# The FFN's first product: every second group of channel tiles by seven block products, activations stationary

## The chip, the cores and the metric

One core of a Trainium2 chip. Its engines run side by side: TensorE (PE in the profile: matmuls; PEld: their weight loads), VectorE (DVE), ScalarE (ACT), GpSimd (POOL) and SyncE (SP, which here only issues transfers from the chip's memory). Each engine executes its own queue of instructions in order; an instruction that needs another engine's result waits at the head of its queue. The metric is the device time of one execution in microseconds: before the change the median of three runs is 1574.26 us (1574.19 to 1574.32).

## The reference, cut to what matters

One layer over 256 tokens of width 2048, in float32. A mixer (recurrent branch, attention, pooling, gates) yields `merged`; then

```
x = x + merged @ w_out
h2 = rms_norm(x, g_ffn)                      # x / rms(x) * g_ffn, per token
gate, up = split(h2 @ w_ffn_in, 2)           # 2048 -> 2 x 5632 channels
x = x + (silu(gate) * up) @ w_ffn_out        # 5632 -> 2048
return rms_norm(x, g_final)
```

Only the part from `w_out` to the end is touched.

## The kernel before

All activations are kept transposed, [128 channels of a tile, 256 tokens]. Products must be near float32 accurate, so each operand is taken as two parts of about 12 bits, `hi` and `lo`, that PE multiplies at full rate, and three of the four partial products are summed: hi.hi, hi.lo, lo.hi.

A weight comes as a piece of 1 MB (`load`, into one of three buffers `raw`). `split` (L69, L70) makes the two parts of 1024 columns of it: ACT casts to `whi`, DVE subtracts to `wlo`; four such pairs of part buffers exist (`hl`), and splits are given priority over up to 200 earlier instructions (`AHEAD`), which fixes where they stand in the queues. In `mm_t` (L82, L83) the weight parts are stationary, 128 x 128 at a time, and the activations move: one matmul of 512 columns (hi and lo of 256 tokens side by side) and one of 256. `mm_n` (L91 to L93) writes the same sum as three matmuls of 256 columns into one half of a bank. `evac_t` adds the two halves of a `mm_t` result (ACT copy L100, DVE add L101).

The order of the stages: v and forget logits; queries, keys and attention; the other branches; gates and merge (`mT`, the merged activations in two parts); out projection (16 tiles, each followed by the residual add and by h2, L578, L579, without the norm's factor, which is applied later); the FFN's first product, 44 channel tiles, each a gate block and an up block of 16 x 128 x 128 (88 loads of `wffi`); the down projection, 16 tiles of 44 x 128 x 128; the last norm, and the store of the result. The norm's factor R2 comes from `rsqrt_mean` (a chain of small operations) and multiplies gate (DVE, L601) and up (POOL, L604); L605 to L607 form the product and its two parts, `act`, for all 44 tiles.

The v stage (L263 to L265) is the one place where activations are stationary and weights move, in blocks of 344 columns. In attention, four transpositions by the identity stand between other products (L338).

Of the kernel before, what the change touches and what calls it, by code (L numbers as in the profile page):

```python
# [7 lines left out]
F32 = mybir.dt.float32  # L8
# [20 lines left out]
GATES = (2, 2, 2, 4)  # merge gates taken between the groups of the two branches  # L29
WARM = 8  # products of constants that run while the first loads are under way  # L30
# [8 lines left out]
def block_kernel(ctx: ExitStack, tc: tile.TileContext, xT, vec,  # L39
# [5 lines left out]
    raw_p = ctx.enter_context(tc.tile_pool(name="raw", bufs=3))  # L45
    hl_p = ctx.enter_context(tc.tile_pool(name="hl", bufs=4))
    acc_p = ctx.enter_context(tc.tile_pool(name="acc", bufs=4, space=bass.MemoryType.PSUM))
    aux_p = ctx.enter_context(tc.tile_pool(name="aux", bufs=4, space=bass.MemoryType.PSUM))
    hT_p = ctx.enter_context(tc.tile_pool(name="hT", bufs=1))
    sm = ctx.enter_context(tc.tile_pool(name="sm", bufs=2))  # L50

# [34 lines left out]
    # the same in columns 0..255 alone: a longer product, a shorter way out  # L86
# [8 lines left out]
    def evac_t(ps, dst, scale=1.0):  # L95
        """Adds the two halves of a transposed product, times scale, into dst [128, 256]."""
# [25 lines left out]
    vhl = at_p.tile([P, 2, 2, DB], F32R, name="vhl", bufs=1)  # token tile, part, channel  # L122
# [5 lines left out]
    warm = aux()  # keeps the array clocked up until the first operands are there  # L128
# [3 lines left out]
    def prepare_x(k):  # L132
        """Contraction tile k of x * g_mix as two parts, and its share of the sum of squares."""
# [12 lines left out]
    def rsqrt_mean(dst, ss, n, pool, nm):  # L146
        """dst (or two factors of it) = (ss / D + eps) ** -0.5, with one Newton step behind the table's root."""
# [45 lines left out]
    for c in (0, 2):  # keep where query >= key  # L193
# [109 lines left out]
    def scores(h, q, k):  # L303
        """Softmax of head h's scores, transposed: [keys 0 | queries 0, 1], [keys 1 | queries 1]."""
# [10 lines left out]
        ns = at_p.tile([P, 3 * P], F32, name="ns")  # minus the scores  # L315
        st = at_p.tile([P, 8], F32, name="st")  # minus the maxima, sums, their reciprocals
# [77 lines left out]
    def lru_in(g):  # L394
# [22 lines left out]
        # gelu(y) = y (1 + tanh(c (y + 0.044715 y^3))) / 2  # L417
# [8 lines left out]
    def lru_out(g, u, uh, ul, ga):  # L426
# [14 lines left out]
        # th = tanh(-log(a) / 2): 1 - a = 2 th / (1 + th), 1 - a^2 = (1 - a)(1 + a).  # L441
# [7 lines left out]
        V.scalar_tensor_tensor(rg, rg, 2.0, rc, ALU.mult, ALU.mult)  # 1 - a  # L449
# [18 lines left out]
    def pool_in(g):  # L468
# [6 lines left out]
        # sums over 2, 4, 8, 16 tokens, each from the one before; column c holds token c - PADW  # L475
# [6 lines left out]
        # the mean, less the token itself: the first tokens count what there is  # L482
# [29 lines left out]
    def gate(n):  # L512
        """Sigmoid of gate block n = 3 m + branch."""
# [21 lines left out]
    mx_p.release()  # L535
    mT_p = tc.alloc_tile_pool(name="mT", bufs=1)
# [23 lines left out]
    h2 = hT_p.tile([P, KD, 2 * T], F32R, name="hT")  # [hi | lo] of x2 * g_ffn, transposed  # L560
# [22 lines left out]
    sg_p.release()
    yAC_p.release()
    yB_p.release()

# [1 line left out]
    ac_p = tc.alloc_tile_pool(name="act", bufs=1)  # L588
    act = ac_p.tile([P, NF, 2 * T], F32R, name="act")
    for f in range(NF):  # L590
        pg = proj_t(wffi[2 * f], lambda k: h2[:, k, :])
        pu = proj_t(wffi[2 * f + 1], lambda k: h2[:, k, :])
        if f == 0:
            ps = aux()
            PE.matmul(ps[:, :T], lhsT=ones, rhs=s2acc, start=True, stop=True)
            R2 = const.tile([P, T], F32, name="R2")
            rsqrt_mean(R2, [ps[:, :T]], T, sm, ("t0", "t1"))
        gt = sm.tile([P, T], F32, name="t0")
        up = sm.tile([P, T], F32, name="t1")
        evac_t(pg, gt)  # L600
        V.tensor_mul(gt, gt, R2)  # L601
        S.activation(gt, gt, AF.Silu)
        evac_t(pu, up)
        G.tensor_mul(up, up, R2)  # L604
        V.tensor_mul(gt, gt, up)  # L605
        S.copy(act[:, f, :T], gt)
        V.tensor_sub(act[:, f, T:], gt, act[:, f, :T].bitcast(F32))  # L607

# [4 lines left out]
    for m in range(KD):  # L613
        ps = acc()
        for a in range(0, NF, 16):
            n = min(16, NF - a)
            r = load(wffo[m, :, a * P:(a + n) * P], n * P)
            for c in range(0, n, 8):
                nk = min(8, n - c)
# [7 lines left out]
                (mm_n if m == last else mm_t)(ps, hi, lo, lambda k, k0=k0: act[:, k0 + k, :], nk,  # L627
                                              k0 == 0, k0 + nk == NF)
        g_ = vecs[:, GL + m:GL + m + 1]
        if m < last:  # L630
            o = sm.tile([P, T], F32, name="t0")
            evac_t(ps, o)
# [93 lines left out]
```

## Time and profile before

| | us |
|---|---|
| median of the runs | 1574.26 |
| span of the profiled execution | 1572.5 |
| first FFN product, 818.4 to 1312.2 | 493.8 |
| down projection, 1312.2 to 1559.4 | 247.2 |
| tail behind the last product, 1559.4 to 1572.5 | 13.1 |

The profile is one execution. Busy shares are of that span, and PE's counts the pipelined matmuls, whose ends are modelled. The profiled execution's own time is its span with 1.8 us around it, taking the runs' median for it. In the chain of what ended last, each step is followed back to what released it.

### The profile page before, as it was taken

To read this page: it belongs to the slowest core of one execution; us is meant where nothing else is said; L and a number is where in the kernel's file an instruction comes from. 1 tells how busy PE (TensorE), PEld (TensorE's weight loads), DVE (VectorE), ACT (ScalarE), POOL (GpSimd) and SP (SyncE) were. 2 spreads that over 40 slices of the span, in tenths; PEclk is the share of its full clock that TensorE was granted. 3 is DMA by queue.
4 is the path that set the end of the run, shared out by engine and by line. 5 is a ranking of instruction groups with operands and counts; after the bars stand their busy time and mean duration, and the time that the engine had idled before them with its cause. 6 is when DMAs were issued, how large, how long until landed. Compare 5 with 4: busy or idle time off the path is not lost.

```text
span 1572.5 us, 22842 instructions
## 1 busy us (share of the span) xinstructions
PE 1549.3 (99%) x8948; PEld 1362.1 (87%) x8948; DVE 994.3 (63%) x1356; ACT 821.3 (52%) x1264; POOL 154.8 (10%) x210
## 2 busy tenths in 40 slices
PE   8999999999999999999999999999999999999997
PEld 8888888888888888888888888888888888888886
DVE  9776677787565656667776555555555555445453
ACT  6565566666444444445555444444444444444442
POOL 7400011102000000000110000000000000010100
PEclk9999999999999999999999999999999999999998
DMA  7444455545555455555555555555555555555552
GB/s 245 170 155 159 140 184 185 212 164 200 185 190 197 167 202 184 201 174 201 188 188 183 189 189 189 188 188 188 188 188 187 188 188 178 188 196 178 192 187 88
DMA packets 46764, 288.92 MB, mean 184 GB/s; under 512 B 5184, under 2 KB 8000, under 8 KB 15936
## 3 DMA queue, kind: packets, MB, share of 16 engines
q1 hardware_dynamic: 46080, 286.54, 52.5%
q8 instruction: 70, 1.15, 0.3%
q10 hardware_dynamic: 576, 0.92, 0.2%
q14 instruction: 38, 0.31, 0.1%
HBM read 285.34 MB, written 2.10 MB: 183 GB/s over the span
## 4 chain that ended last, share of the span: by engine, by line
PE 93%; DVE 2%; POOL 2%; issue 2%; ACT 1%; DMA 0%; SPq 0%; DVEq 0%; POOLq 0%; ACTq 0%
PE acc L82 59%; PE acc L83 30%; POOL xn L232 1%; POOL part L144 1%; DVE wlo L70 1%; ACT whi L69 0%; POOL lev L479 0%; PE acc L91 0%; PE acc L93 0%; PE acc L92 0%; DVE xt L657 0%; PE aux L338 0%; DVE lma L179 0%; PE acc L264 0%; DMA raw<-in_wvf 0%
## 5 line engine op out<-in xcount | busy, mean ns | idle before, releaser
L82 PE MATMUL acc<-hT,whi 128*128 128x512 f32 x2800 | 983.6, 395 | 0.4 <-DVE hT L579 0.4
L70 DVE TENSOR_TENSOR wlo<-raw,whi 128x1024 fp32r<-128x1024 f32 (+2 forms) x554 | 671.3, 1213 | 476.5 <-ACT whi L69 475.5
L69 ACT CAST whi<-raw 128x1024 fp32r<-128x1024 f32 (+2 forms) x554 | 567.9, 1026 | 614.2 <-PE acc L82 425.1
L83 PE MATMUL acc<-hT,wlo 128*128 128x256 f32 x2800 | 785.6, 281 | 0.0
L82 PEld LDWEIGHTS acc<-hT,whi 128*128 128x128 f32 x2800 | 526.3, 188 | 122.2 <-DVE hT L579 0.7
L83 PEld LDWEIGHTS acc<-hT,wlo 128*128 128x128 f32 x2800 | 527.2, 188 | 0.2
L82 PE MATMUL acc<-act,whi 128*128 128x512 f32 x660 | 231.1, 395 | 0.0
L83 PE MATMUL acc<-act,wlo 128*128 128x256 f32 x660 | 185.1, 280 | 0.0
L82 PEld LDWEIGHTS acc<-act,whi 128*128 128x128 f32 x660 | 124.1, 188 | 29.1
L83 PEld LDWEIGHTS acc<-act,wlo 128*128 128x128 f32 x660 | 124.3, 188 | 0.0
L100 ACT COPY evt<-acc 128x256 f32<-128x256 f32 x247 | 90.0, 365 | 0.0
L82 PE MATMUL acc<-mT,whi 128*128 128x512 f32 x256 | 89.8, 395 | 0.0
L604 POOL TENSOR_TENSOR t<-t,R 128x256 f32<-128x256 f32 x44 | 32.4, 737 | 459.3 <-DVE t L101 435.0
L83 PE MATMUL acc<-mT,wlo 128*128 128x256 f32 x256 | 71.6, 280 | 0.0
L101 DVE TENSOR_TENSOR t<-acc,evt 128x256 f32<-128x256 f32 x167 | 69.7, 417 | 1.0 <-ACT evt L100 0.9
L568 POOL TENSOR_TENSOR sacc<-sacc,t 128x256 f32<-128x256 f32 x29 | 34.6, 1195 | 293.0 <-ACT t L567 293.0
L82 PEld LDWEIGHTS acc<-mT,whi 128*128 128x128 f32 x256 | 48.1, 188 | 11.4 <-DVE mT L554 0.3
L83 PEld LDWEIGHTS acc<-mT,wlo 128*128 128x128 f32 x256 | 48.2, 188 | 0.0
L551 POOL TENSOR_TENSOR t<-t,t 128x256 f32<-128x256 f32 x16 | 11.8, 740 | 352.3 <-DVE t L549 352.3
L82 PE MATMUL acc<-yB,whi 128*128 128x512 f32 x128 | 45.5, 395 | 0.0
L82 PE MATMUL acc<-yC,whi 128*128 128x512 f32 x128 | 45.5, 395 | 0.0
L82 PE MATMUL acc<-yA,whi 128*128 128x512 f32 x128 | 45.5, 395 | 0.0
(246 smaller groups left out, 1209.9 us busy)
## 6 DMA issues: line engine op xcount, KB each, us to landing
raw<-in_wffi SPq DMA_DIRECT2D x88, 1024.0 KB, 4.8
raw<-in_wgate SPq DMA_DIRECT2D x48, 1024.0 KB, 4.8
raw<-in_wffo SPq DMA_DIRECT2D x32, 1024.0 KB, 4.9
raw<-in_wqk SPq DMA_DIRECT2D x16, 1024.0 KB, 4.8
raw<-in_wxy SPq DMA_DIRECT2D x16, 1024.0 KB, 4.9
raw<-in_wbr SPq DMA_DIRECT2D x16, 1024.0 KB, 5.0
raw<-in_wout SPq DMA_DIRECT2D x16, 1024.0 KB, 4.8
raw<-in_wffo SPq DMA_DIRECT2D x16, 768.0 KB, 4.3
```

Source lines behind the costliest of these rows:

```text
L69: S.copy(hi[:, :n], r[:, a:a + n])
L70: V.tensor_sub(lo[:, :n], r[:, a:a + n], hi[:, :n].bitcast(F32))
L82: PE.matmul(ps, lhsT=hi[:, w], rhs=rhs(k), start=first and k == 0, stop=False)
L83: PE.matmul(ps[:, :T], lhsT=lo[:, w], rhs=rhs(k)[:, :T], start=False, stop=last and k == nk - 1)
L100: S.copy(tmp, ps[:, T:])
L101: V.tensor_add(dst, ps[:, :T], tmp)
L144: G.tensor_add(part, part, sq)
L232: G.tensor_mul(xn, xt[:, k, :], Rrow)
L551: (G if b == 1 else V).tensor_add(tot, tot, o)
L568: G.tensor_add(sacc, sacc, sq)
L604: G.tensor_mul(up, up, R2)
```

## The change

The two FFN products are written anew.

*Layout.* The result of the first product is now [128 tokens, 256 channels]: activations are stationary (`hs`, for each of 8 tiles of half the contraction eight forms in two parts), weights move, 256 columns at a time (a pair of channel tiles). The contraction of 2048 is halved (a1, a2), the tokens are halved, and gate and up are the two column halves: a product of 2 x 2 blocks. A group is two channel tiles, gate and up: four loads of 1 MB (b11, b21 for gate, b12, b22 for up) in the order b12, b22, b11, b21.

*Plain group* (`group_plain`): eight block products, four loads split in two halves each: 8 x 24 = 192 matmuls of 256 columns.

*Group by seven products* (`group_strassen`): 7 x 24 = 168 matmuls. Sums of weight blocks are made by DVE in float32 before they are split, four additions of 128 x 2048 (L672), so 14 halves are split. Three of the seven products share banks A, B and C with others. `s = B - m1` (L699) reads bank B before the product with b22 accumulates into it. Groups take turns by `PATTERN = (1, 0)`: of 22 groups 11 of each kind, the first by seven products.

*Forms of the activations.* The out projection's stage, from tile 8 on, makes four sums and differences of 128 x 128 blocks and their parts.

*Way back.* `turn` transposes a group's result (four PE transpositions of 128 x 128, float32, L730) one group later and forms `act`'s parts (ACT copy, DVE L733). The norm's factor is now a column per token, taken in by the activation function and by `gated` (L679).

*Chunks.* First product and down projection alternate in chunks of 12, 12, 12 and 8 channel tiles; the down projection is all `mm_n`, and adds straight from the bank to the residual `xt`.

*Memory.* After the out projection, `mT`'s pool and the three raw buffers are given back and six raw buffers (`raw6`) are taken in their place. Banks: six of one result each, two for transpositions.

```
-    raw_p = ctx.enter_context(tc.tile_pool(name="raw", bufs=3))
+    raw_p = tc.alloc_tile_pool(name="raw", bufs=3, side="right")
...
-    mT_p = tc.alloc_tile_pool(name="mT", bufs=1)
+    mT_p = tc.alloc_tile_pool(name="mT", bufs=1, side="right")
...
+    def forms(k, first, src):
+        n = src.shape[1]
+        S.copy(hs[:, k, first:first + n, 0, :], src)
+        V.tensor_sub(hs[:, k, first:first + n, 1, :], src, hs[:, k, first:first + n, 0, :].bitcast(F32))
...
+            forms(k, m // KB * 2, hm)
+            if m >= KB:
+                a11, a21, a12, a22 = hg[:, k, :P], hg[:, k, P:], hm[:, 0, :], hm[:, 1, :]
+                c = hg_p.tile([P, 4, P], F32, name="hc", bufs=2)
+                V.tensor_sub(c[:, 1, :], a11, a21)
+                V.tensor_add(c[:, 2, :], c[:, 1, :], a22)
+                V.tensor_sub(c[:, 3, :], a12, c[:, 2, :])
+                V.tensor_sub(c[:, 0, :], a21, a22)
+                forms(k, 4, c)
...
     mT_p.release()
...
-    for f in range(NF):
-        pg = proj_t(wffi[2 * f], lambda k: h2[:, k, :])
-        pu = proj_t(wffi[2 * f + 1], lambda k: h2[:, k, :])
...
+    raw_p.release()
+    raw_p = tc.alloc_tile_pool(name="raw6", bufs=6, side="right", reuse_waits="tile")
...
+    def parts(r):
+        got = []
+        for h in range(2):
+            w = r[:, :, h * 512:(h + 1) * 512]
+            hi = hl_p.tile([P, 2, 512], F32R, name="whi")
+            lo = hl_p.tile([P, 2, 512], F32R, name="wlo")
+            with tc.high_priority(offset=AHEAD):
+                S.copy(hi, w)
+                V.tensor_sub(lo, w, hi.bitcast(F32))
+            got.append((hi, lo))
+        return got
...
+    def product(ps, ws, forms_, start, stop, more=False):
+        for h, (hi, lo) in enumerate(ws):
+            for o, f in zip(ps, forms_):
+                for part, w in ((0, hi), (1, hi), (0, lo)):
+                    for j in range(4):
+                        k = 4 * h + j
+                        PE.matmul(o, lhsT=hs[:, k, f, part, :], rhs=w[:, :, j * P:(j + 1) * P],
...
+    def blocks(i):
+        src = wffi[4 * i:4 * i + 4].rearrange("(j s) p (h c) -> s h p j c", s=2, h=2)
+        got = {}
+        for s, h in ((1, 0), (1, 1), (0, 0), (0, 1)):
+            got[s, h] = raw()
+            nc.sync.dma_start(got[s, h], src[s, h])
+        return got[0, 0], got[0, 1], got[1, 0], got[1, 1]
...
+    def group_strassen(i):
+        b11, b21, x, b22 = blocks(i)
+        y = raw()
+        add(y, b11, x, ADDS[0])
+        add(x, x, b22, ADDS[1])
+        A, B, C = bank(), bank(), bank()
+        product([C], parts(x), [5], True, True, True)
+        add(x, x, b11, ADDS[2])
+        product([B], parts(y), [4], True, True, True)
+        n5 = tmp("n5")
+        S.copy(n5, B)
+        product([A], parts(b11), [0], True, True, True)
+        m1 = tmp("m1")
+        S.copy(m1, A)
+        product([B], parts(x), [6], False, True, True)
+        add(x, x, b21, ADDS[3])
+        s = tmp("s")
+        V.tensor_sub(s, B, m1)
+        d = tmp("d")
+        V.tensor_sub(d, n5, s)
+        V.tensor_sub(s, s, C)
+        product([A], parts(b21), [2], False, True, True)
+        g0 = tmp("g0")
+        S.activation(g0, A, AF.Silu, scale=r2[:, 0:1])
+        product([B], parts(b22), [7], False, True, True)
+        V.tensor_sub(m1, B, m1)
+        product([C], parts(x), [3], False, True, True)
+        V.tensor_add(d, d, C)
+        S.activation(d, d, AF.Silu, scale=r2[:, 1:2])
+        return gated(0, m1, m1, g0), gated(1, s, s, d)
+    def group_plain(i):
+        b11, b21, b12, b22 = blocks(i)
+        c = [[bank(), bank()] for _ in range(2)]
+        product([c[0][0], c[1][0]], parts(b11), [0, 1], True, False)
+        product([c[0][0], c[1][0]], parts(b21), [2, 3], False, True)
...
+    def turn(a, f):
+        tp = aux_p.tile([P, 2, T], F32, name="turn")
+        for j in range(2):
+            for t in range(2):
+                PE.transpose(tp[:, j, t * P:(t + 1) * P], a[t][:, j * P:(j + 1) * P],
+                             ident.bitcast(F32))
+        S.copy(act[:, f:f + 2, :T], tp)
+        V.tensor_sub(act[:, f:f + 2, T:], tp, act[:, f:f + 2, :T].bitcast(F32))
...
+    for ci, n in enumerate(CHUNKS):
...
+        for f in range(0, n, 2):
+            got = (group_strassen if PATTERN[done % len(PATTERN)] else group_plain)(done)
+            done += 1
+            if late is not None:
+                turn(*late)
+            late = got, f
+        for m in range(KD):
...
+                mm_n(ps, hi, lo, lambda k, c=c: act[:, c + k, :], nk, c == 0, c + nk == n)
+            V.tensor_add(xt[:, m, :], xt[:, m, :], ps)
```

In the rows of the instructions' order that follow, a tile's number tells one buffer's content from another's, and the brackets name the engines or DMA queues whose signals an instruction waits for. First SP's queue where the out projection's last loads (`in_wout`) are followed by the FFN's first (`in_wffi`). Before:

```order
L61 DMA raw_7921<-in_wout 128x2048 [waits DMAHW6_49,DVE_49]
L61 DMA raw_7974<-in_wout 128x2048 [waits DMAHW7_49,DVE_49]
L61 DMA raw_8035<-in_wffi 128x2048 [waits DMAHW0_49,DVE_49]
L61 DMA raw_8078<-in_wffi 128x2048 [waits DMAHW1_49,DVE_49]
L61 DMA raw_8148<-in_wffi 128x2048 [waits DMAHW2_49,DVE_49]
L61 DMA raw_8191<-in_wffi 128x2048 [waits DMAHW3_49,DVE_49]
```

And now:

```order
L63 DMA raw_8056<-in_wout 128x2048 [waits DMAHW7_49,DVE_49]
L663 DMA raw_8156<-in_wffi 128x2x1024 [waits PE_49,Pool_49]
L663 DMA raw_8158<-in_wffi 128x2x1024 [waits DMAHW2_49,DVE_49]
L663 DMA raw_8160<-in_wffi 128x2x1024 [waits DMAHW0_49]
L663 DMA raw_8162<-in_wffi 128x2x1024 [waits DMAHW1_49]
L663 DMA raw_8412<-in_wffi 128x2x1024 [waits Pool_49]
```

The first FFN load waited for its own buffer's last reader on DVE and for a DMA queue; it now waits for PE and POOL, and the loads behind it stand in the same queue.

Then DVE's queue inside the first product. `wlo` is a part of a weight piece (`raw`), `t0`, `t1` a tile's gate and up, `act` the second product's operand. Before, about one channel tile:

```order
L101 TENSOR_TENSOR t0_8333<-acc_8247,evt_8335 128x256 [waits DVE_49,Activation_49]
L601 TENSOR_TENSOR t0_8333<-t0_8333,R2_8122 128x256 [waits DVE_49]
L70 TENSOR_TENSOR wlo_8394<-raw_8391,whi_8393 128x1024 [waits DMAHW2_49,PE_49,Activation_49]
L70 TENSOR_TENSOR wlo_8398<-raw_8391,whi_8397 128x1024 [waits PE_49,Activation_49]
L101 TENSOR_TENSOR t1_8334<-acc_8290,evt_8340 128x256 [waits Activation_49]
L605 TENSOR_TENSOR t0_8333<-t0_8333,t1_8334 128x256 [waits Pool_49]
L70 TENSOR_TENSOR wlo_8451<-raw_8448,whi_8450 128x1024 [waits DMAHW3_49,PE_49,Activation_49]
L607 TENSOR_TENSOR act_8033<-t0_8333,act_8033 128x256 [waits Activation_49]
L70 TENSOR_TENSOR wlo_8455<-raw_8448,whi_8454 128x1024 [waits PE_49,Activation_49]
```

And now, in the second group by seven products, from the fourth big addition on (8663 is x, 8669 b21, 8665 b22, 8675 bank B, 8676 bank C, `turn` a transposed result, 8930 and up the next group's weights):

```order
L672 TENSOR_TENSOR raw_8663<-raw_8663,raw_8669 128x2048 [waits DMAHW6_49,DVE_49]
L642 TENSOR_TENSOR wlo_8817<-raw_8669,whi_8816 128x1024 [waits PE_49,Activation_49]
L642 TENSOR_TENSOR wlo_8821<-raw_8669,whi_8820 128x1024 [waits PE_49,Activation_49]
L642 TENSOR_TENSOR wlo_8851<-raw_8665,whi_8850 128x1024 [waits PE_49,Activation_49]
L642 TENSOR_TENSOR wlo_8855<-raw_8665,whi_8854 128x1024 [waits PE_49,Activation_49]
L642 TENSOR_TENSOR wlo_8884<-raw_8663,whi_8883 128x1024 [waits PE_49,Activation_49]
L642 TENSOR_TENSOR wlo_8888<-raw_8663,whi_8887 128x1024 [waits PE_49,Activation_49]
L699 TENSOR_TENSOR s_8811<-bank_8675,m1_8776 128x256
L733 TENSOR_TENSOR act_8134<-turn_8919,act_8134 128x2x256 [waits Activation_49]
L701 TENSOR_TENSOR d_8813<-n5_8742,s_8811 128x256 [waits DVE_49]
L702 TENSOR_TENSOR s_8811<-s_8811,bank_8676 128x256 [waits DVE_49]
```

The two splits of each weight piece stood between single small operations; now the six last splits of the group's 14 stand in a row behind an addition of 2048 columns, and the subtraction that reads bank B (L699) stands behind them.

## Rows read from the trace of the kernel before

**Rows 1.** The page: busy time of each engine; the chain by engine.
```profile
PE 1549.3 (99%) x8948; PEld 1362.1 (87%) x8948; DVE 994.3 (63%) x1356; ACT 821.3 (52%) x1264; POOL 154.8 (10%) x210
...
PE 93%; DVE 2%; POOL 2%; issue 2%; ACT 1%; DMA 0%; SPq 0%; DVEq 0%; POOLq 0%; ACTq 0%
```

**Rows 2.** Windows: us, then PE, PEld, DVE, ACT, POOL busy, PEclk, DMA, GB/s.
```profile
818.40:1312.20 493.80, 493.39 (x2819) 431.30 (x2818) 298.33 (x403) 243.56 (x356) 32.93 (x45) 1.00 0.54 187
1312.20:1559.40 247.20, 247.20 (x1458) 218.06 (x1456) 117.84 (x126) 109.25 (x142) 20.35 (x15) 1.00 0.52 174
```

**Rows 3.** Groups by form, 850 to 1300: busy us, mean ns | idle before, releaser.
```profile
L70 DVE TENSOR_TENSOR wlo<-raw,whi 128x1024 fp32r<-128x1024 f32 x161 | 197.1, 1224 | 144.0 <-ACT whi L69 144.0
L69 ACT CAST whi<-raw 128x1024 fp32r<-128x1024 f32 x161 | 168.9, 1049 | 224.3 <-issue 119.7 <-PE acc L82 103.1 <-PE acc L83 1.5
L101 DVE TENSOR_TENSOR t<-acc,evt 128x256 f32<-128x256 f32 x81 | 33.8, 417 | 0.0
```

**Rows 4.** Timeline of PE, last down tile: start, us, instruction [idle before].
```profile
1555.49 0.28 PE L91 MATMUL acc<-act,whi 128*128 128x256 f32 x1
...
1559.04 0.28 PE L91 MATMUL acc<-act,whi 128*128 128x256 f32 x1
```

**Rows 5.** Timeline of PE, v stage, weights moving.
```profile
30.05 0.32 PE L265 MATMUL acc<-whi,hT 128*128 128x344 f32 x1
...
33.84 0.32 PE L265 MATMUL aux<-whi,hT 128*128 128x344 f32 x1
```

**Rows 6.** Timeline of DVE in the first FFN product.
```profile
1100.76 1.22 DVE L70 TENSOR_TENSOR wlo<-raw,whi 128x1024 fp32r<-128x1024 f32 x1 [1.58 <-ACT whi L69]
1101.90 0.42 DVE L101 TENSOR_TENSOR t<-acc,evt 128x256 f32<-128x256 f32 x1
```

**Rows 7.** Timeline of the tail.
```profile
1559.27 0.28 PE L93 MATMUL acc<-act,wlo 128*128 128x256 f32 x1
1559.59 0.42 DVE L639 TENSOR_TENSOR xt<-xt,acc 128x256 f32<-128x256 f32 x1 [9.04 <-PE acc L93]
...
1562.44 0.60 DVE L653 TENSOR_SCALAR t<-ident,nr,r3rt 128x128 f32<-128x128 f32 x2
```

**Rows 8.** Tile mT: its last reader (min/median/max ns, first and last start).
```profile
L83 PE MATMUL acc<-mT,wlo x256: 276/280/285, 728.8 to 818.3; 128*128 128x256 f32 x128
```

**Rows 9.** Timeline of SP's queue, 790 to 830.
```profile
798.49 29.29 SPq L61 DMA_DIRECT2D raw<-in_wffi  x6
```

**Rows 10.** The page: DMA issues, KB each, median us from issue to landing.
```profile
raw<-in_wffi SPq DMA_DIRECT2D x88, 1024.0 KB, 4.8
```

**Rows 11.** Windows (columns as in rows 2), the first loads.
```profile
10.00:14.00 4.00, 4.00 (x15) 3.78 (x14) 3.90 (x4) 3.86 (x8) 4.00 (x4) 1.00 1.04 394
```

**Rows 12.** Timeline of PE: products of constants; transpositions between products.
```profile
1.06 3.78 PE L130 MATMUL aux<-ones 128*128 128x128 f32 x16 [1.06 <-POOL ones L126]
...
104.60 0.39 PE L82 MATMUL acc<-hT,whi 128*128 128x512 f32 x1
104.83 0.29 PE L338 MATMUL aux<-ident,ph 128*128 128x128 f32 x2
104.95 0.35 PE L83 MATMUL acc<-hT,wlo 128*128 128x256 f32 x1
105.14 0.39 PE L82 MATMUL acc<-hT,whi 128*128 128x512 f32 x1
```

**Rows 13.** Windows (columns as in rows 2), the out projection.
```profile
728.60:818.40 89.80, 89.80 (x514) 78.31 (x513) 64.74 (x82) 48.96 (x79) 14.54 (x15) 1.00 0.54 187
```

**Rows 14.** Windows (columns as in rows 2), the v stage.
```profile
9.00:10.00 1.00, 1.00 (x5) 1.00 (x4) 1.00 (x2) 0.93 (x1) 1.00 (x2) 1.00 1.06 371
18.00:19.00 1.00, 1.00 (x4) 1.00 (x5) 1.00 (x3) 0.00 (x0) 0.00 (x0) 0.50 0.13 25
24.00:25.00 1.00, 1.00 (x8) 1.00 (x7) 1.00 (x2) 0.68 (x3) 0.48 (x1) 1.00 0.73 219
```

**Rows 15.** Timeline of PE, v stage, behind idle times.
```profile
8.13 0.66 PE L264 MATMUL acc<-wlo,hT 128*128 128x344 f32 x1 [1.73 <-DVE wlo L70]
...
17.95 0.66 PE L264 MATMUL acc<-wlo,hT 128*128 128x344 f32 x1 [3.89 <-DVE wlo L70]
```

More of the change, by code (lines that the diff above doesn't have):

```diff
@@ L29 @@
 GATES = (2, 2, 2, 4)
+PATTERN = (1, 0)
+ADDS = ("v", "v", "v", "v")
+CHUNKS = (12, 12, 12, 8)
 WARM = 8
@@ L44, in block_kernel @@
     const = ctx.enter_context(tc.tile_pool(name="const", bufs=1))
[L45 removed]
     hl_p = ctx.enter_context(tc.tile_pool(name="hl", bufs=4))
[L47 to L49 removed]
+    acc_p = tc.alloc_tile_pool(name="acc", bufs=4, space=bass.MemoryType.PSUM)
+    aux_p = tc.alloc_tile_pool(name="aux", bufs=4, space=bass.MemoryType.PSUM)
     sm = ctx.enter_context(tc.tile_pool(name="sm", bufs=2))
+    raw_p = tc.alloc_tile_pool(name="raw", bufs=3, side="right")
     def acc():
@@ L111, in proj_t @@
         return ps
-    hT = hT_p.tile([P, KD, 2 * T], F32R, name="hT")
     vecs = const.tile([P, NV], F32, name="vecs")
@@ L117, in block_kernel @@
     xt = x_p.tile([P, KD, T], F32, name="xt")
+    hT_p = tc.alloc_tile_pool(name="hT", bufs=1)
+    hT = hT_p.tile([P, KD, 2 * T], F32R, name="hT")
     yB_p = tc.alloc_tile_pool(name="yB", bufs=1)
@@ L557, in block_kernel @@
                 gate(len(sigs))
-    h2 = hT_p.tile([P, KD, 2 * T], F32R, name="hT")
+    sg_p.release()
+    yAC_p.release()
+    yB_p.release()
+    hT_p.release()
+    hs_p = tc.alloc_tile_pool(name="hs", bufs=1)
+    hs = hs_p.tile([P, KB, 8, 2, P], F32R, name="hs")
+    hg_p = tc.alloc_tile_pool(name="hg", bufs=1)
+    hg = hg_p.tile([P, KB, T], F32, name="hg")
     def squares(m, sacc):
@@ L574, in block_kernel @@
         evac_t(ps, o)
-        g_ = vecs[:, GF + m:GF + m + 1]
+        k = m % KB
         with tc.high_priority(offset=AHEAD):
             V.tensor_add(xt[:, m, :], xt[:, m, :], o)
-            S.activation(h2[:, m, :T], xt[:, m, :], AF.Copy, scale=g_)
-            V.scalar_tensor_tensor(h2[:, m, T:], xt[:, m, :], g_, h2[:, m, :T].bitcast(F32),
-                                   ALU.mult, ALU.subtract)
+            hm = hg[:, k, :] if m < KB else hg_p.tile([P, T], F32, name="hm", bufs=2)
+            S.activation(hm, xt[:, m, :], AF.Copy, scale=vecs[:, GF + m:GF + m + 1])
+            hm = hm.rearrange("p (a b) -> p a b", a=2)
+            forms(k, m // KB * 2, hm)
[7 more added lines that the diff above has]
+                forms(k, 4, c)
@@ L581, in block_kernel @@
         squares(m, s2acc)
+    hg_p.release()
     mT_p.release()
[L583 to L589, printed above, removed]
-    for f in range(NF):
-        pg = proj_t(wffi[2 * f], lambda k: h2[:, k, :])
-        pu = proj_t(wffi[2 * f + 1], lambda k: h2[:, k, :])
[L593 to L607, printed above, removed]
+    raw_p.release()
@@ new lines, in block_kernel, with bank @@
+    raw_p = tc.alloc_tile_pool(name="raw6", bufs=6, side="right", reuse_waits="tile")
+    aux_p.release()
+    acc_p.release()
+    acc_p = tc.alloc_tile_pool(name="bank", bufs=6, space=bass.MemoryType.PSUM, reuse_waits="tile")
+    aux_p = tc.alloc_tile_pool(name="turn", bufs=2, space=bass.MemoryType.PSUM, reuse_waits="tile")
+    act_p = tc.alloc_tile_pool(name="act", bufs=1)
+    act = act_p.tile([P, max(CHUNKS), 2 * T], F32R, name="act")
+    ft_p = tc.alloc_tile_pool(name="ft", bufs=2)
+    def bank():
+        return acc_p.tile([P, T], F32, name="bank")
@@ new lines, in raw @@
+    def raw():
+        return raw_p.tile([P, 2, 1024], F32, name="raw")
+    def parts(r):
[16 more added lines that the diff above has]
+                        PE.matmul(o, lhsT=hs[:, k, f, part, :], rhs=w[:, :, j * P:(j + 1) * P],
+                                  start=start and h == 0 and part == 0 and w is hi and j == 0,
+                                  stop=stop and h == 1 and w is lo and j == 3, skip_group_check=more)
@@ new lines, in blocks, with add @@
+    def blocks(i):
[5 more added lines that the diff above has]
+        return got[0, 0], got[0, 1], got[1, 0], got[1, 1]
+    def add(dst, a, b, how):
+        with tc.high_priority(offset=AHEAD):
+            if how == "dma":
+                G.dma_start(dst, b, accum_op=ALU.add)
+            else:
+                V.tensor_add(dst, a, b)
@@ new lines, in tmp, with gated @@
+    def tmp(nm):
+        return ft_p.tile([P, T], F32, name=nm)
+    def gated(t, a, up, g):
+        V.scalar_tensor_tensor(a, up, r2[:, t:t + 1], g, ALU.mult, ALU.mult)
+        return a
+    def group_strassen(i):
[28 more added lines that the diff above has]
+        return gated(0, m1, m1, g0), gated(1, s, s, d)
@@ new lines, in group_plain @@
+    def group_plain(i):
[3 more added lines that the diff above has]
+        product([c[0][0], c[1][0]], parts(b21), [2, 3], False, True)
+        g = [tmp("g0"), tmp("d")]
+        for t in range(2):
+            S.activation(g[t], c[t][0], AF.Silu, scale=r2[:, t:t + 1])
+        product([c[0][1], c[1][1]], parts(b12), [0, 1], True, False)
+        product([c[0][1], c[1][1]], parts(b22), [2, 3], False, True)
+        return [gated(t, tmp(("m1", "s")[t]), c[t][1], g[t]) for t in range(2)]
@@ new lines, in turn @@
+    def turn(a, f):
+        tp = aux_p.tile([P, 2, T], F32, name="turn")
+        for j in range(2):
+            for t in range(2):
+                PE.transpose(tp[:, j, t * P:(t + 1) * P], a[t][:, j * P:(j + 1) * P],
+                             ident.bitcast(F32))
+        S.copy(act[:, f:f + 2, :T], tp)
+        V.tensor_sub(act[:, f:f + 2, T:], tp, act[:, f:f + 2, :T].bitcast(F32))
+    pss = [aux_p.tile([P, 2, T], F32, name="turn")[:, 0, :1] for _ in range(2)]
+    for t in range(2):
+        PE.matmul(pss[t], lhsT=s2acc[:, t * P:(t + 1) * P], rhs=ones[:, :1], start=True, stop=True)
@@ L610, in block_kernel @@
+    r2a, r2b = rsqrt_mean(None, pss, 2, const, ("r2ms", "r2rt"))
+    r2 = const.tile([P, 2], F32, name="r2")
+    V.tensor_mul(r2, r2a, r2b)
     s3acc = const.tile([P, T], F32, name="sacc")
@@ L612, in block_kernel @@
     last = KD - 1
[L613 to L619, printed above, removed]
-                hi, lo = split(r, c * P, nk * P)
-                k0 = a + c
-                if m == last and k0 == 32:
-                    pss = [aux()[:, :1] for _ in range(2)]
+    f0 = done = 0
+    for ci, n in enumerate(CHUNKS):
+        final = ci == len(CHUNKS) - 1
+        late = None
+        for f in range(0, n, 2):
[5 more added lines that the diff above has]
+        for m in range(KD):
+            ps = acc_p.tile([P, T], F32, name="bank")
+            r = raw_p.tile([P, 2048], F32, name="raw")
+            nc.sync.dma_start(r[:, :n * P], wffo[m, :, f0 * P:(f0 + n) * P])
+            for c in range(0, n, n // 2):
+                nk = n // 2
+                hi, lo = split(r, c * P, nk * P)
+                if late is not None and c:
+                    turn(*late)
+                    late = None
+                if final and m == last and c:
+                    pss = [aux_p.tile([P, 2, T], F32, name="turn")[:, 0, :1] for _ in range(2)]
                     for t in range(2):
@@ L626, in block_kernel @@
                                   start=True, stop=False)
[L627 to L632, printed above, removed]
-            V.tensor_add(xt[:, m, :], xt[:, m, :], o)
-            squares(m, s3acc)
-            S.activation(xt[:, m, :], xt[:, m, :], AF.Copy, scale=g_)
-            if m == last // 2:
-                S.sqrt(rcol3, s3acc[:, :2])
-        else:
-            V.tensor_add(xt[:, m, :], xt[:, m, :], ps[:, :T])
-            sq = sm.tile([P, T], F32, name="t1")
-            S.square(sq, xt[:, m, :])
-            S.activation(xt[:, m, :], xt[:, m, :], AF.Copy, scale=g_)
+                mm_n(ps, hi, lo, lambda k, c=c: act[:, c + k, :], nk, c == 0, c + nk == n)
+            V.tensor_add(xt[:, m, :], xt[:, m, :], ps)
+            if final:
+                g_ = vecs[:, GL + m:GL + m + 1]
+                if m < last:
+                    squares(m, s3acc)
+                else:
+                    sq = sm.tile([P, T], F32, name="t1")
+                    S.square(sq, xt[:, m, :])
+                S.activation(xt[:, m, :], xt[:, m, :], AF.Copy, scale=g_)
+                if m == last // 2:
+                    S.sqrt(rcol3, s3acc[:, :2])
+        f0 += n
     for t in range(2):
@@ L649, in block_kernel @@
     diag = sm.tile([P, T], F32, name="t0")
-    R3 = aux()
+    R3 = aux_p.tile([P, 2 * T], F32, name="turn")
     for t in range(2):
@@ L660, in block_kernel @@
             (nc.sync if m % 4 else S).dma_start(out[:, first:m + 1, :], xt[:, first:m + 1, :])
-    ac_p.release()
+    raw_p.release()
+    ft_p.release()
+    act_p.release()
+    hs_p.release()
+    aux_p.release()
+    acc_p.release()
 def _blocks(w, k):
```

## The prediction

> **What bounds the kernel now.** I read the page's first part and its chain first: TensorE (PE) is busy 1549.3 of 1572.5 us, and 93% of the chain that ended last is PE [rows 1]. So only what PE has to do, or has to wait for, moves the end. Next the stretches of the two FFN products [rows 2]: the first takes 493.8 us and the second 247.2, with PE busy all through and a granted clock of 1.00, while VectorE (DVE) is busy 298 us (60%) and ScalarE (ACT) 244 us of the first. PE waits for nobody there; the others wait for it: ACT's weight casts stood 103.1 us for a buffer that PE still read [rows 3]. So taking columns from PE gains, and any new wait of PE costs in full. Last the tail from 1559.4 to the end, 13.1 us, in which PE does next to nothing.
>
> **Prices.** A 256-column matmul with its own weights, issued back to back: 30 intervals lie between the two rows of [rows 4], 3.55/30 = .1183 us. The first product of before makes 44 x 2 x 16 = 1408 pairs (512 and 256 columns): 493.8/1408 = .3507, or .1169 for 256 columns. With activations stationary and weights moving the kernel has one place, of 344 columns: 24 intervals in 3.79 us [rows 5], .1579, by columns .1175 for 256; if the 88 further columns took one cycle of 2.4 GHz each (.037), .1213. I take .1183, the row nearest in shape, and .1169 and .1213 as ends. A split of 1024 columns costs ACT 1.05 and DVE 1.22, a 256-column addition .42 [rows 3]; back to back, DVE goes on 1.14 after a split started [rows 6]. A straight line through 256 and 1024 columns gives the 2048-column weight add 2.30 us, 2.22 from start to start; the trace has none, so bounds of 2.1 (the line's slope alone) and 3.6 (half as dear again, should two full fp32 operands cost more than these). From a matmul's end of issue (1559.27 + .12) to DVE's start .20 [rows 7]. Half a weight block, 12 matmuls, is 1.42 us of PE.
>
> **The change, term by term**, from 818.4 us, where the last out-projection matmul ends [rows 8].
>
> 1. Start of the FFN. Before, its first loads were issued from 798.49 on, 20 us ahead [rows 9]. Now the new pool of raw pieces lies where mT lay: the first wffi load waits for PE, I take it for the last matmul that reads mT, and four more loads stand behind it in SP's queue. A 1 MB load lands 4.8 us after its issue [rows 10]; at 394 GB/s [rows 11] 2.7 of that is transfer, 2.1 latency. The first sum needs loads 1 and 3: .2 + 2.1 + 3.15 MB at 394 GB/s (8.0) = 10.3, then two adds 4.4, an ACT cast 1.05 and hand-overs: 16.1 us without a product. The second norm's chain of small operations (alike in the tail: 1559.59 to 1562.44, 2.9 us [rows 7]) lies beside that. Bounds 14 and 21, from cheap and dear adds and the transfer.
> 2. First Strassen group. DVE is the slower here: 13 splits 14.8, two more adds 4.4, the difference s .4, waits 1.1: s ends 20.7 after PE's start, .1 to PE, then the last four halves 5.7: 26.5.
> 3. Eleven plain groups: 192 x .1183 = 22.7 each, 249.8. Their eight splits (9.1 us of DVE) fit beside that.
> 4. Seven steady Strassen groups, each behind a plain one. PE has 14 halves, 168 matmuls, 19.9 us. But the eleventh half (b22) accumulates into bank B, which DVE must first read for s; and in DVE's queue s stands behind the splits of *all* the remaining halves and the fourth big add. When the plain group ends, at T, the four part buffers hold at most the first four halves. So ahead of s are still 11 splits 12.5, a product with the norm's factor .34, the subtraction on a transposed result .61 (512 columns by the same line), the add 2.2, s itself .4: 16.1; with .2 for the wake-up and 1.4 for buffers that PE gives back half by half, s ends at T + 17.7. PE has by then done ten halves, 14.2, and four transposes, .5, and stands idle for 3. So 17.8 + 5.7 = 23.5 each, 164.5. Even a DVE that never was late would leave a wait: the fourteenth half's split needs the buffer of the tenth, so s ends .2 + 1.05 + 1.2 + .4 after PE has finished b21: 2.9, with .5 of transposes in it.
> 5. Three Strassen groups that open a later chunk; their first four halves are split during the down projection. The first buffer is back at 1.42 + .2, then a cast 1.05, ten splits 11.4, the add 2.2, s .4: 16.7, and 5.7: 22.4 each, 67.2.
> 6. Chunk ends: the transposes of the last two groups have no wait to lie in: 2 x .5 and .3 for the results, 1.3 x 4 = 5.2. A transposition: two f32r ones lengthened a step of .35 to .54 (104.60 to 105.14 [rows 12]), .10 each; eight fp32 products of 128 columns, each recorded as two instructions, took 3.78 us [rows 12], .24 each if that was at half clock. I take .12, a set of four .5; with .24 a set is .95, and some fifteen sets stand in PE's way: up to +7.
>
> The first product is thus 16.1 + 26.5 + 249.8 + 164.5 + 67.2 + 5.2 = 529.3, +35.5.
>
> 7. Down projection: 44 x 16 x 3 = 2112 matmuls of 256 columns, 249.8 against 247.2: +2.6. Its residual adds come straight out of PSUM beside PE.
> 8. Out projection: from tile 8 on four DVE operations of 128 columns (.2 each) and one of 512 (.6) more, 1.4 us a tile; of 89.8 us DVE was free for 25.1 [rows 13], 1.6 a tile: nothing, +4 if each of those tiles held PE by half a microsecond. Tail: the same operations, 13.1. POOL's products and ACT's evacuations go, off the path.
>
> Sum: 1572.5 + 35.5 + 2.6 = 1610.6 of span. The median shown stands 1.8 above the profiled span: **1612**.
>
> The Trainium skill, "TensorE: Matmul & The Clock Gate", section "Part 4: PE-mode transpose", gives about 275 ns for a transposition inside a kernel. No run here shows it yet; by that price, an estimate, a set costs 1.1 and the sum would rise by some 9.
>
> **Rivals.**
> A. *PE stays the bound*: the loads come early and DVE is never late. Then 11 x (22.7 + 19.9) + 22 x .5 = 479.6, 14.2 under before, +2.6: 1563. For it: DVE's mean load, 22 splits, four adds and some ten small ones, about 38 us for a pair of groups that takes PE 42.6. Against it: DVE's order, and the buffer that s hangs on. It decides whether s ends within 14.7 us of the plain group's end. .05.
> B. *The first load's wait is an early one*, for an older matmul: the loads land beside the out projection and term 1 shrinks to the adds or less: 1598. .10.
> C. *TensorE's clock falls at each wait*. Early on PE stood for 3.89 us before 17.95 [rows 15] and the granted clock was .50 until about 24 [rows 14]: 6 us at 1.2 GHz, 3 lost; after 1.73 us of idling before 8.13 it stayed at 1.00. The waits here, about 3 us and .5 of transposes, lie between. Ten of them x 3.0: 1642. .16.
> That section of the Trainium skill also says that transposes don't count as work for the clock; by that the .5 us would belong to the idle time. No row here has a transposition in an idle stretch.
> D. *Upper prices*: transposes at .24 (+7), .1213 for the 2112 matmuls of plain groups, some 500 last ones of Strassen groups and the down projection (+14), or adds of 3.6, one a group on the path (+14): one or two of these give 1619 to 1633. .11.
>
> **How the numbers follow.** The forecast as worked out, its own range 1600 to 1625, has .58; with A to D that is 1. Slower by over 0.2% (3.1 us, about what a measurement of this kernel can tell from no change) are B, C, D and the forecast but for a remnant, .92; faster is A with a part of the remnant, .06; .02 lies between. The range takes in D, most of B, and reaches up to C: 1594 to 1642.
>
> **What will show it.** PE idle for about 16 us before the FFN's first matmul (line 653), the wffi load issued at 818 and not 798; PE's wait for DVE's s (line 699), 2 to 3 us in each of eleven groups; L653 spaced .118; the adds (line 672) about 2.3 us; PEclk 1.00 right behind those waits; POOL's L604 gone; the down projection some 250 us in four parts. A first product under 500 us would prove terms 1 and 4 wrong; a PEclk of .5 behind the waits would prove C.

## The result, and the profile after

The changed kernel took 1631.05 us (median of four runs, 1630.66 to 1632.31), the kernel before 1574.22: a ratio of 1.0362 (95% interval 1.0347 to 1.0376). Forecast: 1612, range 1594 to 1642.

The page of the changed kernel, its busy time and chain, for comparison with [rows 1]:

```profile
PE 1558.8 (96%) x10842; PEld 1460.1 (90%) x10842; DVE 1165.2 (71%) x1473; ACT 882.4 (54%) x1283; POOL 114.8 (7%) x166
...
PE 88%; DVE 6%; issue 2%; POOL 2%; ACT 1%; DMA 1%; POOLq 0%; DVEq 0%; SPq 0%; ACTq 0%
```

PE's share fell from 99% to 96%, and DVE now holds 6% of the chain instead of 2%. What PE waited for (us in total, times, longest):

```profile
PE bank L653 <- DVE s L699: 31.1, 11, 3.8
PE bank L653 <- ACT whi L641: 12.7, 1, 12.7
PE turn L737 <- POOL sacc L581: 3.2, 1, 3.2
```

The first two waits are those of the forecast. The third, for the second norm's product, lies in the same idle time at the start, ahead of the 12.7. The FFN has no other wait but one of .5 for the last norm's product, in the last down tile. The timeline of PE, the first matmul, then the first, the second (steady) and a chunk-opening wait for s:

```profile
834.67 2.07 PE L653 MATMUL bank<-whi,hs 128*128 128x256 f32 x8 [12.68 <-ACT whi L641]
855.52 2.04 PE L653 MATMUL bank<-whi,hs 128*128 128x256 f32 x8 [3.80 <-DVE s L699]
904.27 1.18 PE L653 MATMUL bank<-whi,hs 128*128 128x256 f32 x8 [2.50 <-DVE s L699]
952.14 1.24 PE L653 MATMUL bank<-whi,hs 128*128 128x256 f32 x8 [2.49 <-DVE s L699]
1068.40 1.42 PE L653 MATMUL bank<-whi,hs 128*128 128x256 f32 x8 [3.30 <-DVE s L699]
```

SP's queue shows the start's cause, against [rows 9]:

```profile
818.25 2.77 SPq L663 DMA_DIRECT2D raw<-in_wffi  x5
```

The loads are issued at 818.25, not at 798.49. And DVE's timeline ahead of the wait that ends at 952.14:

```profile
942.55 2.29 DVE L672 TENSOR_TENSOR raw<-raw 128x2048 f32<-128x2048 f32 x1
944.76 6.90 DVE L642 TENSOR_TENSOR wlo<-raw,whi 128x1024 fp32r<-128x1024 f32 x6
951.57 0.42 DVE L699 TENSOR_TENSOR s<-bank,m 128x256 f32<-128x256 f32 x1
```

The fourth add, six splits without a gap, then s; bank B had been complete since about 946, where PE had finished the product with x. What the forecast had wrong stands in the windows (columns as in [rows 2]) right behind the waits, and further on:

```profile
855.50:862.30 6.80, 6.78 (x37) 6.80 (x38) 3.23 (x6) 2.38 (x3) 0.00 (x0) 0.60 0.71 270
904.30:910.30 6.00, 6.00 (x38) 6.00 (x39) 3.80 (x6) 2.55 (x3) 0.00 (x0) 0.72 0.74 300
910.30:949.60 39.30, 39.30 (x332) 39.11 (x331) 33.35 (x30) 22.70 (x26) 0.00 (x0) 1.00 0.43 142
```

Behind each wait the granted clock averaged .72 over 6 us (a part of them at .50), so 6.0 x .28 = 1.7 us are lost there, and 6.8 x .40 = 2.7 behind the first wait.

### The profile page after: what moved, and what is told of

It reads as the page before. It is cut to its first block, busy times and chain, and to the rows that moved or that the text cites. A ratio compares the mean times of both kernels' runs of the same rounds, so it can differ in the third digit from the quotient of the medians.

```text
span 1630.6 us, 26772 instructions
## 1 busy us (share of the span) xinstructions
PE 1558.8 (96%) x10842; PEld 1460.1 (90%) x10842; DVE 1165.2 (71%) x1473; ACT 882.4 (54%) x1283; POOL 114.8 (7%) x166
## 4 chain that ended last, share of the span: by engine, by line
PE 88%; DVE 6%; issue 2%; POOL 2%; ACT 1%; DMA 1%; POOLq 0%; DVEq 0%; SPq 0%; ACTq 0%
PE bank L653 28%; PE acc L84 28%; PE acc L85 14%; PE bank L94 5%; PE bank L93 5%; PE bank L95 5%; DVE wlo L642 3%; POOL part L147 1%; POOL xn L235 1%; DMA raw<-in_wffi 1%; PE turn L730 0%; POOL lev L482 0%; DVE wlo L72 0%; ACT whi L641 0%; DVE xt L797 0%
## 5 line engine op out<-in xcount | busy, mean ns | idle before, releaser
L72 DVE TENSOR_TENSOR wlo<-raw,whi 128x1024 fp32r<-128x1024 f32 (+4 forms) x410 | 461.1, 1126 | 281.5 <-ACT whi L71 278.0
L71 ACT CAST whi<-raw 128x1024 fp32r<-128x1024 f32 (+4 forms) x410 | 389.2, 951 | 380.3 <-PE acc L84 197.8
L84 PE MATMUL acc<-hT,whi 128*128 128x512 f32 x1392 | 491.1, 396 | 0.0
L653 PE MATMUL bank<-whi,hs 128*128 128x256 f32 x2640 | 382.6, 289 | 43.8 <-DVE s L699 31.1
L653 PEld LDWEIGHTS bank<-whi,hs 128*128 128x128 f32 x2640 | 350.4, 196 | 46.0 <-issue 33.2
L85 PE MATMUL acc<-hT,wlo 128*128 128x256 f32 x1392 | 391.3, 281 | 0.0
L642 DVE TENSOR_TENSOR wlo<-raw,whi 128x1024 fp32r<-128x1024 f32 x242 | 289.6, 1222 | 84.1 <-ACT whi L641 82.6
L85 PEld LDWEIGHTS acc<-hT,wlo 128*128 128x128 f32 x1392 | 262.7, 189 | 0.2
L653 PE MATMUL bank<-wlo,hs 128*128 128x256 f32 x1320 | 217.1, 288 | 0.0
L93 PE MATMUL bank<-act,whi 128*128 128x256 f32 x704 | 197.4, 281 | 0.0
L94 PE MATMUL bank<-act,whi 128*128 128x256 f32 x704 | 197.2, 280 | 0.0
L653 PEld LDWEIGHTS bank<-wlo,hs 128*128 128x128 f32 x1320 | 186.8, 196 | 0.0
L94 PEld LDWEIGHTS bank<-act,whi 128*128 128x128 f32 x704 | 132.8, 189 | 0.4 <-DVE act L733 0.2
L93 PEld LDWEIGHTS bank<-act,whi 128*128 128x128 f32 x704 | 132.3, 188 | 0.2 <-ACT act L732 0.2
L672 DVE TENSOR_TENSOR raw<-raw 128x2048 f32<-128x2048 f32 x44 | 100.8, 2290 | 6.1 <-DMA raw<-in_wffi 5.0
```

The source lines that it names most:

```text
L84: PE.matmul(ps, lhsT=hi[:, w], rhs=rhs(k), start=first and k == 0, stop=False)
L85: PE.matmul(ps[:, :T], lhsT=lo[:, w], rhs=rhs(k)[:, :T], start=False, stop=last and k == nk - 1)
L93: PE.matmul(o, lhsT=hi[:, w], rhs=rhs(k)[:, :T], start=first and k == 0, stop=False)
L94: PE.matmul(o, lhsT=hi[:, w], rhs=rhs(k)[:, T:], start=False, stop=False)
L642: V.tensor_sub(lo, w, hi.bitcast(F32))
L653: PE.matmul(o, lhsT=hs[:, k, f, part, :], rhs=w[:, :, j * P:(j + 1) * P], start=start and h == 0 and part == 0 and w is hi and j == 0, sto ...
```

## Experiments

All times are medians beside the kernel before on the same chip (1574.2 to 1574.6).

**1. s ahead of the last splits.**

```
-        V.tensor_sub(s, B, m1)
+        with tc.high_priority(offset=AHEAD):
+            V.tensor_sub(s, B, m1)
```

> Only the place of one DVE instruction changes: the subtraction that reads bank B (s) is given the splits' priority, so that DVE does it behind the splits of b21 and ahead of the four last ones. Theory (PE's wait is DVE's order, and the clock falls because of the wait): s is ready before PE has finished b21, the wait of about 2.5 us goes from ten groups and 3.8 from the first, and with it the half clock behind each (3.4 us at half speed, 1.7 lost): 1631 - 10 x 4.2 - about 4 = 1585 us, mean granted clock back near .99, PE's wait for s gone. Rival (DVE is as late with the last splits as it was with s): PE waits for the splits of b22 instead, the clock still falls, 1615 to 1630.

Measured: 1585.07 (1.0068, 1.0053 to 1.0083). DVE's timeline has s between b21's and b22's splits, and PE goes on without a wait behind its transpositions:

```profile
891.25 2.35 DVE L642 TENSOR_TENSOR wlo<-raw,whi 128x1024 fp32r<-128x1024 f32 x2
893.53 0.42 DVE L700 TENSOR_TENSOR s<-bank,m 128x256 f32<-128x256 f32 x1
```

```profile
898.65 0.27 PE L731 MATMUL turn<-ident,s 128*128 128x128 f32 x1
898.68 1.18 PE L653 MATMUL bank<-whi,hs 128*128 128x256 f32 x8
```

One instruction's place cost 46 us, wait and clock together.

**2. The b22 product in a bank of its own**, s where it was.

```
-        product([B], parts(b22), [7], False, True, True)
+        product([E], parts(b22), [7], True, True, True)
         V.tensor_sub(m1, B, m1)
+        V.tensor_add(m1, m1, E)
```

> The product with b22 goes to a bank of its own and is added by one more DVE operation of 256 columns; s keeps its place behind all splits, and PE has nothing to wait for there. Theory as for the reordered s: about 1585 us, PE's wait for s gone, PEclk 1.00 there, although DVE does s later than before. Rival (the groups by seven products are bound by DVE's total, so that another wait opens at once): 1610 or more, with waits of PE for splits in the next plain group or at b22.

Measured: 1585.86 (1.0069, 1.0053 to 1.0086), no wait of PE for s. In the second group PE goes on with b22 at 898.59, and DVE does s only behind that:

```profile
898.59 1.18 PE L653 MATMUL bank<-whi,hs 128*128 128x256 f32 x8
```

```profile
899.03 0.41 DVE L699 TENSOR_TENSOR s<-bank,m 128x256 f32<-128x256 f32 x1
```

So it is PE's dependence on s that costs, not the time at which DVE does s, nor DVE's total.

**3. Useless matmuls in the wait.**

```
+        ws = parts(b22)
+        for j in range(20):
+            PE.matmul(E, lhsT=hs[:, j % 8, 7, 0, :], rhs=ws[0][0][:, :, j % 4 * P:(j % 4 + 1) * P],
+                      start=True, stop=True)
-        product([B], parts(b22), [7], False, True, True)
+        product([B], ws, [7], False, True, True)
```

> Twenty matmuls of 256 columns with no use (2.4 us, into a bank that nobody reads) stand in PE's queue just ahead of the product with b22, in the time in which PE waited; the wait for s stays what it was. Theory (the half clock behind the wait is the wait's doing): PE has work in the wait, the clock stays at 1.00, each group gains the 1.7 us lost at half clock and the first some 2.5: 1631 - 19 = 1612 us, the same as the forecast without a fall of the clock. Rival (the slow stretch belongs to something else, as the groups' buffers or the start of b22): 1631 or up to 1635, clock .976.

Measured: 1615.61 (1.0264, 1.0248 to 1.0279), 15.4 under the change. The six microseconds from b22 on in the second group:

```profile
902.70:908.70 6.00, 5.99 (x50) 5.99 (x51) 5.10 (x8) 4.23 (x5) 0.00 (x0) 1.00 0.76 307
```

1.00 in place of .72, although b22 starts 3.0 us after the tenth half against 3.1 in the change: the slow stretch is the idle time's doing. Only the first group, with 2.27 us of waiting left, still lost clock. Its first eight matmuls behind the wait took 2.07 us, where the second group's take 1.21:

```profile
854.96 2.07 PE L653 MATMUL bank<-whi,hs 128*128 128x256 f32 x8 [2.27 <-DVE s L699]
```

**4. Plain groups alone** (`PATTERN = (0,)`).

> All 22 groups as eight products, no sums of weight blocks, everything else as in the change. Theory: no wait for s anywhere, clock 1.00; the start is idle for 16.5 - two adds of 2.2 = 12 us; 22 x (22.75 + .44 for the transposes) = 510; ends of chunks 1; down projection +2.6: 1574.2 - 493.8 + 12 + 510 + 1 + 2.6 = 1606 us, so that the seven products as they stand cost 25 us against plain ones. Rival (a group by seven products is worth its 24 matmuls even with its wait): 1631 or more.

Measured: 1607.34 (1.0208, 1.0193 to 1.0224). As the change orders it, taking out 11 x 24 matmuls made the kernel 24 us longer. With s ahead (run 1) the same seven products are 22 us faster than plain groups, 1585.07 against 1607.34.

**5. Old raw buffers kept**, s ahead as in 1.

```
-    raw_p.release()
-    raw_p = tc.alloc_tile_pool(name="raw6", bufs=6, side="right", reuse_waits="tile")
+    raw2_p = tc.alloc_tile_pool(name="raw2", bufs=3, side="right", reuse_waits="tile")
+    def next_raw():
+        taken[0] += 1
+        return (raw_p if (taken[0] - 1) % 6 < 3 else raw2_p).tile([P, RAW], F32, name="raw")
```

> The kernel with s moved ahead (1585.1 us), and besides that the three raw buffers of the earlier stages are kept and three new ones taken in mT's place, used in turn as six; so the FFN's first three loads (b12, b22, b11) go into old buffers and don't wait for mT's last reader. Theory (16.5 us at the start are the wait for mT, the transfer of three loads, two adds and a cast): the loads are there before the out projection ends, and of the idle time only the sum y into a new buffer, the sum x, the cast remain: .2 + 2.3 + 2.3 + 1.1 = 6: 1585 - 10.5 = 1574.5 us. Rival (the second norm's chain or the forms of the last channel tile set the start): idle time of 13 or more, 1582 to 1586.

Measured: 1611.9 (1.0246, 1.023 to 1.0261): the expectation failed, though its own term came out. The first matmul on PE's timeline starts 10.8 us earlier than in 1 (834.86), and then new waits appear:

```profile
824.03 0.58 PE L657 MATMUL bank<-whi,hs 128*128 128x256 f32 x1 [5.99 <-ACT whi L645]
...
899.98 1.19 PE L657 MATMUL bank<-whi,hs 128*128 128x256 f32 x8 [1.63 <-DVE s L707]
903.90 1.56 PE L657 MATMUL bank<-whi,hs 128*128 128x256 f32 x11 [0.71 <-ACT whi L645]
```

The wait of 5.99 is the forecast 6. One new wait is the second norm's: its product now stands inside the first group, and PE stood 4.60 for POOL's sum.

```profile
835.29 1.01 PE L742 MATMUL turn<-ones,sacc 128*128 128x1 f32 x4 [4.60 <-POOL sacc L581]
```

The steady groups' waits go with DVE's order, which moved with the buffers. In 1 the next plain group's first two splits stand ahead of the small operations on a group's result; here they stand behind `d + C`, which waits for the group's last product:

```
898 L714 TENSOR_TENSOR d_8812<-d_8812,bank_8675 128x256 [waits PE_49]
899 L646 TENSOR_TENSOR wlo_8938<-raw_8929,whi_8937 128x1024 [waits DMAHW3_49,Activation_49]
```

```profile
903.12 0.42 DVE L714 TENSOR_TENSOR d<-d,bank 128x256 f32<-128x256 f32 x1 [2.29 <-PE bank L657]
903.88 2.36 DVE L646 TENSOR_TENSOR wlo<-raw,whi 128x1024 fp32r<-128x1024 f32 x2 [0.34 <-ACT whi L645]
```

DVE idles 2.29 us for PE, then PE for DVE, and both carry the delay into the next group. This is read from order and trace; that the order alone does it was not tried apart.

**6. Plain group first**, with s ahead and a plain group's loads in the order of use (`PATTERN = (0, 1)`).

> The kernel with s moved ahead, and the order of the groups turned round (the plain one first, the loads of a plain group in the order in which they are used), raw buffers as in the change. Theory: the first group waits for one load and a cast, .2 + 2.1 + 2.7 + 1.1 = 6.2 instead of 16.5 us, the first group by seven products no longer waits for its sums, and no chunk begins with one: 1585 - 10.3 - 1 = 1573.5 us. Rival (chunks that now end in a group by seven products wait for its longer chain of results before the down projection): 3 us more at each of four ends, 1585.

Measured: 1577.68 (1.0021, 1.0012 to 1.0031), 4 more than expected. PE starts at 824.04, as worked out; the chunk ends cost nothing (waits of .24); the rest lies in the first chunk, where the clock is low after the start (.69 on the mean from 824 to 830) and four waits of .40 to .54 follow.

**7. Together**: 6, the old raw buffers, and the second norm's matmuls behind the first blocks' products.

> Everything together: s ahead, plain groups first, old raw buffers kept, and the second norm's two matmuls behind the first two blocks' products. Theory: no idle time at the start, PE bound through the FFN: 818.2 + 11 x 22.75 + 11 x 19.95 + 22 x .4 + 4 us of chunk ends + 249.8 + 13.1 and 1.8 around: 1565 us, .6% under the kernel before: the gain that 11 x 24 matmuls fewer promise, less moving weights and transposes. Rival (DVE, at 38 us of work in 42.6, is late somewhere with everything else tight, or the clock falls at chunk ends): 1572 or more.

Measured: 1566.34 (.9951, .9935 to .9968): .5% under the kernel before, and 1.3 us above the expectation. SP issues the first FFN load at 797.71, PE's timeline passes from the out projection into the FFN without a gap, and the whole FFN is one stretch of full PE and full clock:

```profile
817.64 0.28 PE L85 MATMUL acc<-mT,wlo 128*128 128x256 f32 x1
817.75 1.11 PE L657 MATMUL bank<-whi,hs 128*128 128x256 f32 x8
```

```profile
817.70:1549.50 731.80, 730.57 (x6154) 726.76 (x6152) 575.45 (x614) 405.43 (x496) 11.98 (x16) 1.00 0.55 185
```

Before, the same work took 493.8 + 247.2 = 741.0 [rows 2].

**8. The fourth add left out.**

> The change with the fourth sum of weight blocks left out (x'' is not formed, so the last product of a group takes the wrong sum): DVE has 2.2 us less ahead of s. Theory as forecast (even a DVE that is never late leaves a wait, because the last split needs the parts' buffer of the tenth half): the wait for s goes from 2.5 to about 1.9 us only, the clock goes on falling in most groups: 1631 - 11 x .6 = 1624 us. Rival (only DVE's amount of work ahead of s counts): the wait falls to .3, the clock stays, 1631 - 11 x 3.9 = 1588.

Measured: 1584.76 (two runs; 1.0068, 1.0048 to 1.0088), no wait for s but the first (2.55), and behind that one the clock stayed at 1.00 (the timeline of PE, then the window, columns as in [rows 2]):

```profile
853.52 1.18 PE L653 MATMUL bank<-whi,hs 128*128 128x256 f32 x8 [2.55 <-DVE s L698]
```

```profile
853.50:859.50 6.00, 5.98 (x51) 6.00 (x52) 4.44 (x7) 3.67 (x4) 0.00 (x0) 1.00 0.78 304
```

So a wait as long as those that slowed the clock in the change did not slow it here: its length alone does not decide, and what else does stays open. The floor that I had forecast did not show. But the order moved too: with 2.2 us less for DVE, s was placed behind the split of the eleventh half, not the fourteenth. So the run does not tell what the buffer alone would cost with s kept last. It does tell that the place of s is itself a result of DVE's load.

## Why the prediction came out as it did

The direction and the mechanism were right; one choice, among the rivals, was wrong. The sum's own range ended at 1625; that 1631 lies inside the range given is owed to rival C's end of it.

| from 818.2 on, us | forecast | measured |
|---|---|---|
| idle at the start (1) | 16.1 | 16.5 |
| first Strassen group: s ready / whole (2) | 20.8 / 26.5 | 20.85 / 29.05 |
| plain group (3) | 22.7 | 22.8 |
| steady group: s ready / last four halves (4) | 17.8 / 5.7 | 17.8 / 7.3 |
| chunk-opening group: s ready / last four halves (5) | 16.8 / 5.7 | 17.7 / 7.3 |
| down projection with a set of transpositions each (7) | 249.8 + 2 | 251.7 |

(From the timeline's starts; the steady group's are: plain group before it ends 886.51, b22 904.27, next group 911.55. Down projection: 3 x 68.2 + 47.1.)

- *Term 1, the start*: right in size and cause; run 5 shows the wait for mT apart.
- *Terms 2, 4, 5, the wait for s*: right to .1 us in the steady groups, .9 too low in the three chunk-opening ones (2.7 in all). There I had let DVE begin free, with ten splits to do behind the first buffer given back. Its timeline around the group's start at 1050.72 has hardly a gap: the third big add runs on into the group, twelve splits follow up to s, and a residual add stands among them.

```profile
1049.34 2.29 DVE L672 TENSOR_TENSOR raw<-raw 128x2048 f32<-128x2048 f32 x1
1051.55 4.63 DVE L642 TENSOR_TENSOR wlo<-raw,whi 128x1024 fp32r<-128x1024 f32 x4
1056.09 0.42 DVE L771 TENSOR_TENSOR xt<-xt,bank 128x256 f32<-128x256 f32 x1
1056.42 2.36 DVE L642 TENSOR_TENSOR wlo<-raw,whi 128x1024 fp32r<-128x1024 f32 x2
```

  Runs 1 and 2 show that the wait is the dependence and its place in DVE's order.
- *The price of the big add*: 2.29 against 2.30 from the line.
- *What failed: "The waits here, about 3 us and .5 of transposes, lie between", and the clock taken as staying.* Rival C was true at half its price: 2.55 at the first wait, 1.6 behind each of the ten others, 18.6 us, which is nearly all of the 19 between forecast and result. I had carried 6 us at half speed over from [rows 14]; here the slow stretch was shorter. Run 3 shows the clock apart from the wait. With .16 for C I stood too low, and ten repetitions made the choice the largest open term. One of the two rows that I leaned on was also misread. That the clock "stayed at 1.00" behind the 1.73 us of idling is what [rows 14] print, but PE's pace before and after the 3.89 us, and later, says otherwise:

```profile
9.16 0.49 PE L265 MATMUL acc<-whi,hT 128*128 128x344 f32 x1
9.44 0.49 PE L264 MATMUL acc<-wlo,hT 128*128 128x344 f32 x1
...
18.70 0.49 PE L264 MATMUL acc<-wlo,hT 128*128 128x344 f32 x1
18.98 0.49 PE L265 MATMUL acc<-whi,hT 128*128 128x344 f32 x1
...
24.23 0.32 PE L264 MATMUL acc<-wlo,hT 128*128 128x344 f32 x1
24.38 0.32 PE L265 MATMUL acc<-whi,hT 128*128 128x344 f32 x1
```

  The same matmul comes every .28 us at 9, as at 18.7 where the view has .50, and every .15 at 24, where it has 1.00. At 9 PE went at half pace whatever the view prints there, so the 1.73 us was no example of an idle time without a slow stretch behind it.
- *The floor*, "even a DVE that never was late would leave a wait", was not tested: run 8 has another order. The change's own trace bears it out. Ahead of the wait that ends at 952.14, ACT's cast of the last half could begin only when PE had read that buffer:

```profile
948.77 1.05 ACT L641 CAST whi<-raw 128x1024 fp32r<-128x1024 f32 x1 [0.38 <-PE bank L653]
```

  It ended at 949.82. A split of 1.22 and s of .42 behind it would end at about 951.5 (an estimate from these rows), while PE was ready at 949.65: some 1.8 of the 2.49, against 2.4 in the forecast.
- *Rival A* (PE stays the bound) is what run 7 reached: 1566.3 against its 1563.
- *Pace and transpositions*: L653 keeps .1186 (22.78/192); four transpositions start .11 apart, and behind the first of a set the next product starts .35 later (886.51 to 886.86). The Trainium skill's 275 ns ("TensorE: Matmul & The Clock Gate", "Part 4: PE-mode transpose") is the recorded duration here, .27; issued back to back they cost PE .11 each, and by the measurement the 9 us fall away.

## What to carry to other kernels

Saved TensorE work can be lost to a new wait: when an accumulation must wait for a read by another engine, look what stands in that engine's queue ahead of the read, and move the read or give the next product its own bank. A wait of 2.5 us on TensorE cost 4.2 in the steady groups here, as the clock fell behind it, though one of 2.55 in run 8 cost no clock: carry the fall as a term of its own, above all for repeated waits. And after any change of buffers or of an engine's load read the order anew: in runs 5 and 8 it moved with them, and in run 5 relief in one place put other operations behind a wait.

## What the runs showed of the hardware

The granted clock fell behind each of the ten idle times of 2.5 to 3.3 us, in a kernel that had run at 1.00 for forty microseconds before; in run 3 it stayed at 1.00 through three of .8. It fell behind the first group's wait of 2.27 in run 3 and not behind the first group's of 2.55 in run 8, so the length of an idle time does not settle it alone.
